# The first input load of a top-2 dispatch kernel, issued as 16 and 112 partitions

## Chip, core and metric

The kernel runs on one core of a Trainium2 chip. A core has five engines, each with its own instruction stream. Three of them matter here: VectorE (DVE), which does all the arithmetic on large tiles; ScalarE (ACT), which computes two sigmoids and issues one store; and SyncE (SP), which computes nothing and issues all the other transfers. A transfer is carried out by 16 DMA engines between HBM and the on-chip memory (SBUF), which has 128 partitions. The metric is device time in microseconds (us) of one execution; lower is better.

## Reference

For each of 16 x 1024 tokens the kernel takes eight router logits, keeps the two largest, turns them into two weights that add up to one, and writes the token's row of 512 floats twice, once scaled by each weight.

```python
def reference(x, router_logits, k):            # x: 16 x 1024 x 512 f32, logits: 16 x 1024 x 8, k = 2
    logits_max = np.max(router_logits, axis=-1, keepdims=True)
    probs = np.exp(router_logits - logits_max)
    probs = probs / np.sum(probs, axis=-1, keepdims=True)
    topk_indices = np.argsort(probs, axis=-1)[..., -k:]
    topk_probs = np.take_along_axis(probs, topk_indices, axis=-1)
    topk_probs = topk_probs / np.sum(topk_probs, axis=-1, keepdims=True)
    x_expanded = x[:, :, np.newaxis, :].repeat(k, axis=2)
    return (x_expanded * topk_probs[..., np.newaxis]).astype(np.float32)
```

The input has 16384 rows of 2 KB (33.6 MB), the output twice as much (67.1 MB), the logits 0.5 MB.

## The kernel before

The 16384 tokens are 128 partitions times 128 rows, in two groups: group 0 has 65 rows in each partition, group 1 has 63 (`GROUPS`). Within a group a partition's rows are neighbours in HBM, so that a load of n rows is, for each partition, one piece of n x 2 KB.

One SBUF buffer, `xs`, holds a group's rows: 65 rows of 512 floats in every partition. A second one, `osp`, holds 18 output rows (each is a pair); at the start it also serves as room for the logits and the work on them. `WA` holds the two weights of every token.

Group 0 is loaded in three transfers of 6, 28 and 31 rows (`LOADS`, line 120). After the first of them the two logits loads are issued (lines 125 and 126), and then the remaining two. All five go out from SP, one behind the other, on SP's DMA queue; none of them waits for anything. Each covers all 128 partitions.

`top2_weights` works on the logits of all tokens at once: a small tournament on DVE (lines 26 to 36), and two sigmoids on ACT of the difference between best and second best (lines 37 and 38). Line 133 then multiplies a block of rows by both weights, into `osp` or into those parts of `xs` whose rows are already used, and line 145 stores the block. The first block is three rows; its store goes out from ACT's queue, all others from SP's. SP's instructions are in program order: five loads, four stores of group 0, three loads of group 1, four stores of group 1. Loads of group 1 wait until the stores that read the same part of `xs` have landed. A multiply waits for its rows' load and for the store that last read its place.

The compiler adds the semaphores. A DMA tells of its landing through one, and there are eight of them that the transfers use in turn.

Of the kernel before, what the change touches and what calls it, by code (L numbers as in the profile page):

```python
# [1 line left out]

# [4 lines left out]

F32 = mybir.dt.float32
ALU = mybir.AluOpType
ACTF = mybir.ActivationFunctionType  # L10
P = 128


def top2_weights(nc, WA, dlt, room, logits, E):

    tt = nc.vector.tensor_tensor
    hi, lo, n = None, None, E  # L20
    while n > 1:
        n //= 2
        if hi is None:
            a, b = logits[:, :, 0:n], logits[:, :, n : 2 * n]
            nhi, nlo = room(n), b
            tt(nhi, a, b, op=ALU.max)  # L26
            tt(nlo, a, b, op=ALU.min)  # L27
        else:
            a, b = hi[:, :, 0:n], hi[:, :, n : 2 * n]
            nhi, nlo, tmp = room(n), room(n), room(n)  # L30
            tt(tmp, lo[:, :, 0:n], lo[:, :, n : 2 * n], op=ALU.max)  # L31
            tt(nlo, a, b, op=ALU.min)  # L32
            tt(nlo, nlo, tmp, op=ALU.max)  # L33
            tt(nhi, a, b, op=ALU.max)  # L34
        hi, lo = nhi, nlo
    tt(dlt, hi[:, :, 0], lo[:, :, 0], op=ALU.subtract)  # L36
    nc.scalar.activation(WA[:, :, 0], dlt, ACTF.Sigmoid, scale=-1.0)  # L37
    nc.scalar.activation(WA[:, :, 1], dlt, ACTF.Sigmoid, scale=1.0)  # L38

GROUPS = [65, 63]

LOADS = [[6, 28, 31], [16, 16, 31]]
BASE = [0, 1]

STORES = [
    [(0, 3, "osp", 0), (3, 15, "osp", 3), (18, 16, "xs", 0), (34, 15, "osp", 0), (49, 16, "xs", 33)],
    [(0, 16, "osp", 2), (16, 16, "xs", 0), (32, 15, "osp", 0), (47, 16, "xs", 32)],
]  # L50

L = 18

FREE = [3, 2]


@with_exitstack
def kernel(
    ctx: ExitStack,
    tc: tile.TileContext,  # L60
    x: bass.AP,
    router_logits: bass.AP,
    k: bass.AP,
    out: bass.AP,
):
    nc = tc.nc
    B, S, D = x.shape
    E = router_logits.shape[-1]
    N = B * S
    assert int(k) == 2 and E == 8 and N == P * sum(GROUPS)  # L70
    M = N // P

    x_v, o_v, rl_v = [], [], []
    t0 = 0
    for n in GROUPS:
        t1 = t0 + P * n
        x_v.append(
            x.rearrange("b s d -> (b s) d")[t0:t1].rearrange("(p m) d -> p m d", p=P)
        )
        o_v.append(  # L80
            out.rearrange("b s k d -> (b s) k d")[t0:t1].rearrange(
                "(p m) k d -> p m k d", p=P
            )
        )
        rl_v.append(
            router_logits.rearrange("b s e -> (b s) e")[t0:t1].rearrange(
                "(p m) e -> p m e", p=P
            )
        )
        t0 = t1  # L90

    wpool = ctx.enter_context(tc.tile_pool(name="wpool", bufs=1))
    xs = wpool.tile([P, max(GROUPS), D], F32)
    osp = wpool.tile([P, L, 2, D], F32)
    WA = wpool.tile([P, M, 2], F32)
    dlt = wpool.tile([P, M], F32)


    flat = osp.rearrange("p l k d -> p (l k d)")
    taken = [0]  # L100

    def room(n):
        o = taken[0]
        taken[0] += M * n
        return flat[:, o : o + M * n].rearrange("p (m n) -> p m n", n=n)

    logits = room(E)

    def place(where, at, n):

        if where == "osp":
            return osp[:, at : at + n]
        return xs[:, at : at + 2 * n, :].rearrange("p (r k) d -> p r k d", k=2)

    m0 = 0
    for g, G in enumerate(GROUPS):
        x0, r = BASE[g], 0
        for n in LOADS[g]:
            tc.keep_in_program_order(
                nc.sync.dma_start(xs[:, x0 + r : x0 + r + n, :], x_v[g][:, r : r + n, :])  # L120
            )
            r += n
            if g == 0 and r == 6:
                n0 = GROUPS[0]
                tc.keep_in_program_order(nc.sync.dma_start(logits[:, :n0], rl_v[0]))  # L125
                tc.keep_in_program_order(nc.sync.dma_start(logits[:, n0:], rl_v[1]))  # L126
                top2_weights(nc, WA, dlt, room, logits, E)
        assert r == G
        for r, n, where, at in STORES[g]:
            og = place(where, at, n)  # L130
            again = where == "osp" and at == 0 and r > 0
            for a, b in [(0, FREE[g]), (FREE[g], n)] if again else [(0, n)]:
                nc.vector.tensor_tensor(  # L133
                    og[:, a:b],
                    xs[:, x0 + r + a : x0 + r + b, :]
                    .unsqueeze(2)
                    .to_broadcast([P, b - a, 2, D]),
                    WA[:, m0 + r + a : m0 + r + b, :]
                    .unsqueeze(3)
                    .to_broadcast([P, b - a, 2, D]),  # L140
                    op=ALU.mult,
                )

            queue = nc.scalar if g == r == 0 else nc.sync
            tc.keep_in_program_order(queue.dma_start(o_v[g][:, r : r + n], og))  # L145
        m0 += G


# [1 line left out]
_INS = ['x', 'router_logits', 'k']  # L150
_OUTS = [((16, 1024, 2, 512), 'float32')]

_NUMBERS = {'k': 2}


# [26 lines left out]
```

## Time and profile before

| What | us |
|---|---|
| median of 3 runs | 239.84 (239.83 to 239.98) |
| the profiled execution's own time | 239.92 |
| its span, from the first to the last instruction | 238.1 |
| DVE busy | 141.9 |
| ACT busy | 1.8 |
| first load: issued at | 0.72 |
| first load: from issue to landing | 6.0 |
| first DVE instruction on logits starts | 8.14 |
| first multiply starts | 12.61 |

The span is what the profile sees of one execution; its own time has 1.8 us more around it. An engine's busy time is the time its instructions ran. For the 16 DMA engines the page gives a share of time in which they had a packet in work, by queue and by slice of the span. A packet is one partition's piece of a transfer: 12 KB in the first load (6 rows), 56 and 62 KB in the next two.

The profile names transfers by the queue that issued them: q1 is SP's, q10 is ACT's.

### The profile page before, as it was taken

How to read it: one execution, taken by the hardware profiler on the slowest of the kernel's cores; microseconds unless marked ns; L12 is line 12 of the kernel's file. 1: busy time of each engine (PE TensorE's matmuls, PEld its weight loads, DVE VectorE, ACT ScalarE, POOL GpSimd, SP SyncE). 2: the span in 40 equal slices, each digit the busy share in tenths (PEclk: the TensorE clock that was granted, in tenths of full speed). 3: DMA queues.
4: the chain of work that ended last, by engine and by line, in shares of the span. 5: the costliest groups of instructions: out<-in, count | busy, mean ns of one | idle time of the engine just before them, and what ended most of it. 6: DMA issues, size and time to landing. Idle time of an engine off the chain costs nothing.

```text
span 238.1 us, 102 instructions
## 1 busy us (share of the span) xinstructions
DVE 141.9 (60%) x22; ACT 1.8 (1%) x3; POOL 0.2 (0%) x4
## 2 busy tenths in 40 slices
DVE  0650499999699999100000699999406999950000
ACT  2000000000000000000000000000000000000000
POOL 0000000000000000000000000000000000000000
DMA  7979998979999999989899999898989999989894
GB/s 265 550 337 500 430 418 374 506 330 495 429 429 407 473 423 402 495 352 528 352 440 435 435 446 501 352 495 374 506 374 462 418 407 451 475 351 517 352 528 176
DMA packets 2448, 101.19 MB, mean 425 GB/s; under 512 B 272, under 2 KB 400, under 8 KB 528
## 3 DMA queue, kind: packets, MB, share of 16 engines
q1 hardware_dynamic: 2304, 99.62, 97.2%
q10 hardware_dynamic: 144, 1.57, 1.5%
HBM read 34.08 MB, written 67.11 MB: 425 GB/s over the span
## 4 chain that ended last, share of the span: by engine, by line
DMA 48%; DVE 40%; SPq 1%; issue 0%; DVEq 0%
DMA xs<-in_x_dram 26%; DVE osp L133 25%; DMA out_dram<-osp 22%; DVE xs L133 14%; SPq L125 0%; SPq L126 0%; SPq L120 0%; SPq L145 0%; DVEq L133 0%
## 5 line engine op out<-in xcount | busy, mean ns | idle before, releaser
L133 DVE TENSOR_TENSOR osp<-xs,WA 128x3072 f32<-128x3072 f32 (+5 forms) x7 | 69.4, 9908 | 61.6 <-DMA xs<-in_x_dram 47.5
L133 DVE TENSOR_TENSOR xs<-xs,WA 128x16384 f32<-128x16384 f32 x4 | 68.9, 17224 | 0.1
L26 DVE TENSOR_TENSOR osp<-osp 128x512 f32<-128x512 f32 x1 | 0.7, 692 | 8.1 <-DMA osp<-in_router_logits_dram 8.1
L37 ACT ACT_TABLE_LOAD x1 | 1.3, 1283 | 0.7 <-PEq L163 0.7
L27 DVE TENSOR_TENSOR osp<-osp 128x512 f32<-128x512 f32 x1 | 0.7, 691 | 0.0
L34 DVE TENSOR_TENSOR osp<-osp 128x256 f32<-128x256 f32 (+1 forms) x2 | 0.7, 352 | 0.0
L32 DVE TENSOR_TENSOR osp<-osp 128x256 f32<-128x256 f32 (+1 forms) x2 | 0.7, 352 | 0.0
L31 DVE TENSOR_TENSOR osp<-osp 128x256 f32<-128x256 f32 (+1 forms) x2 | 0.7, 352 | 0.0
L33 DVE TENSOR_TENSOR osp<-osp 128x256 f32<-128x256 f32 (+1 forms) x2 | 0.7, 351 | 0.0
L37 ACT ACTIVATE WA<-dlt 128x128 f32<-128x128 f32 x1 | 0.3, 314 | 10.1 <-DVE dlt L36 10.1
L36 DVE TENSOR_TENSOR dlt<-osp 128x128 f32<-128x128 f32 x1 | 0.3, 291 | 0.0
L38 ACT ACTIVATE WA<-dlt 128x128 f32<-128x128 f32 x1 | 0.3, 298 | 0.0
L163 POOL MEMSET const-bfloat16-1.0<- 128x1 bf16 x1 | 0.1, 101 | 0.0
L163 POOL MEMSET const-uint8-127<- 128x1 uint8 x1 | 0.1, 101 | 0.0
L163 POOL MEMSET const-float32-0.0<- 128x1 f32 x1 | 0.1, 98 | 0.2 <-issue 0.2
L163 POOL MEMSET const-float32-1.0<- 128x1 f32 x1 | 0.1, 98 | 0.0
## 6 DMA issues: line engine op xcount, KB each, us to landing
out_dram<-osp SPq DMA_DIRECT2D x3, 7680.0 KB, 23.4
xs<-in_x_dram SPq DMA_DIRECT2D x2, 7936.0 KB, 41.7
xs<-in_x_dram SPq DMA_DIRECT2D x2, 4096.0 KB, 40.4
xs<-in_x_dram SPq DMA_DIRECT2D x1, 7168.0 KB, 24.8
xs<-in_x_dram SPq DMA_DIRECT2D x1, 1536.0 KB, 6.0
out_dram<-osp ACTq DMA_DIRECT2D x1, 1536.0 KB, 24.8
osp<-in_router_logits_dram SPq DMA_DIRECT2D x1, 260.0 KB, 6.2
osp<-in_router_logits_dram SPq DMA_DIRECT2D x1, 252.0 KB, 6.4
```

What stands on the lines that cost most here:

```text
L26: tt(nhi, a, b, op=ALU.max)
L27: tt(nlo, a, b, op=ALU.min)
L31: tt(tmp, lo[:, :, 0:n], lo[:, :, n : 2 * n], op=ALU.max)
L32: tt(nlo, a, b, op=ALU.min)
L33: tt(nlo, nlo, tmp, op=ALU.max)
L34: tt(nhi, a, b, op=ALU.max)
L36: tt(dlt, hi[:, :, 0], lo[:, :, 0], op=ALU.subtract)
L37: nc.scalar.activation(WA[:, :, 0], dlt, ACTF.Sigmoid, scale=-1.0)
L38: nc.scalar.activation(WA[:, :, 1], dlt, ACTF.Sigmoid, scale=1.0)
L133: nc.vector.tensor_tensor(og[:, a:b], xs[:, x0 + r + a : x0 + r + b, :] .unsqueeze(2) .to_broadcast([P, b - a, 2, D]), WA[:, m0 + r + a : ...
L163: nc = _bacc.Bacc("TRN2", target_bir_lowering=False, num_devices=1)
```

## The change

The first load of six rows becomes two transfers: one to partitions 0 to 15, then one to partitions 16 to 127. Both go out from SP, in that order, ahead of the logits loads. The other loads are as before.

```diff
         for n in LOADS[g]:
-            tc.keep_in_program_order(
-                nc.sync.dma_start(xs[:, x0 + r : x0 + r + n, :], x_v[g][:, r : r + n, :])
-            )
+
+            parts = [(0, 16), (16, P)] if g == r == 0 else [(0, P)]
+            for p0, p1 in parts:
+                tc.keep_in_program_order(
+                    nc.sync.dma_start(
+                        xs[p0:p1, x0 + r : x0 + r + n, :], x_v[g][p0:p1, r : r + n, :]
+                    )
+                )
             r += n
```

In the built program SP has one instruction more (16 x 3072 and 112 x 3072 elements where 128 x 3072 stood); lines behind it move down by five (133 becomes 138, 145 becomes 150). The order on every engine is otherwise the same. The transfers behind the first use the next semaphore each, and the first multiply, which waited for the one load, waits for the two.

## The prediction, made before the changed kernel was run

> **What bounds the kernel now.** I read the page's DMA part first, since DVE is busy for only 60% of the span.
>
> ```profile
> span 238.1 us, 102 instructions
> ...
> DMA  7979998979999999989899999898989999989894
> ...
> q1 hardware_dynamic: 2304, 99.62, 97.2%
> q10 hardware_dynamic: 144, 1.57, 1.5%
> HBM read 34.08 MB, written 67.11 MB: 425 GB/s over the span
> ```
>
> The reader is to see the two shares: 97.2% + 1.5% = 98.7% of what 16 engines have in 238.1 us, which is 235.0 us of work for each of them. Only 3.1 us are not transfer. Stretches of time (length, then busy time of DVE, ACT and POOL with the count of instructions, clock, DMA share, GB/s) show where those lie:
>
> ```profile
> 0.00:1.73 1.73, 0.00 (x0) 1.01 (x1) 0.20 (x4) 1.00 0.00 0
> 1.73:6.73 5.00, 0.00 (x0) 0.28 (x1) 0.00 (x0) 1.00 0.99 369
> ...
> 60.00:120.00 60.00, 33.78 (x4) 0.00 (x0) 0.00 (x0) 1.00 1.02 443
> 120.00:180.00 60.00, 36.65 (x3) 0.00 (x0) 0.00 (x0) 1.00 1.00 430
> ...
> 237.00:238.10 1.10, 0.00 (x0) 0.00 (x0) 0.00 (x0) 1.00 0.00 0
> ```
>
> Nothing moves before 1.73 us and after 237; in between the share is 1 (a packet counts where it starts, so a stretch can show 1.02). The trace's records of single packets say the same more sharply: first packet at 1.73, last end at 236.94, a mean of 235.11 us of packets on an engine, and 0.09 us per engine in which it had none. So the end is set by 16 engines that never rest: **time = start 1.73 + the packets of the slowest engine + 1.2 for the last landing**. The chain of waits mixes DMA and DVE by turns, and agrees in that each DVE wait in it is for a transfer:
>
> ```profile
> DMA 48%; DVE 40%; SPq 1%; issue 0%; DVEq 0%
> ```
>
> The start, in order of time (start, length, instruction):
>
> ```profile
> 0.72 0.37 SPq L120 DMA_DIRECT2D xs<-in_x_dram  x1
> 1.15 0.43 SPq L125 DMA_DIRECT2D osp<-in_router_logits_dram  x1
> 1.62 0.42 SPq L126 DMA_DIRECT2D osp<-in_router_logits_dram  x1
> 2.09 0.99 SPq L120 DMA_DIRECT2D xs<-in_x_dram  x2
> 8.14 0.69 DVE L26 TENSOR_TENSOR osp<-osp 128x512 f32<-128x512 f32 x1 [8.14 <-DMA osp<-in_router_logits_dram]
> ...
> 12.61 3.36 DVE L133 TENSOR_TENSOR osp<-xs,WA 128x3072 f32<-128x3072 f32 x1 [0.58 <-ACT WA L38]
> ```
>
> All five loads are issued by 3.08, long before the first has landed (0.72 + 6.0 = 6.7). From there the queue is never empty. Each engine has eight 12 KB packets of the first load: the first takes 0.56 to 1.37 us, the other seven 0.46, one every 0.457. Then the logits' packets follow within 10 ns.
>
> **The change, part by part.**
>
> *Removed and added issues.* One SP issue of 0.37 becomes two; the second costs 0.42 (the rows of 0.43 and 0.42 behind the first), and logits and larger loads are issued 0.42 to 0.47 later. The cover is the queue: the logits' packets are wanted at 6.03, and their issue ends at 2.05 now, about 2.5 then. The second part of the first load is wanted sooner. It takes the place of the issue at 1.15; with the first load's distance from issue to first packet, 1.73 - 0.72 = 1.01, its packets can start at 2.16. The engines' first packets end between 2.5 and 3.1. Cost 0. If that cover were gone it would be 0.42.
>
> *Packets.* 128 in both cases, eight for an engine if 16 and 112 partitions are dealt evenly over 16 engines (1 + 7). Bytes are the same. One landing notice more for each engine: the trace has such packets of 4 bytes, 9 ns each. Cost 0.01.
>
> *The added wait* stands at the first multiply (L133, L138 afterwards). It waits till 12.6 for the weights, 5.9 after the load landed; the ten other blocks are queued behind it on DVE, and ACT's store waits for it. With 5.9 us of cover it costs 0; without cover, what the second part is late.
>
> *Which engine writes which partition.* Here I see the only price. Now every transfer of the program spans 128 partitions, and each engine has eight of them; in every such transfer all 16 run together at 12288 B / 460 ns = 26.7 GB/s. The trace cannot tell whose pace that is: the engine's, or that of a lane into the eight partitions it serves. If it is the lane's, a split that makes engines share a lane is paid for. Bounds, from this one row. First part: 16 packets over n lanes take 16/n x 0.457. With n = 16 that is 0.46, as now, and the extra is 0; with sixteen neighbours on two lanes of eight (n = 2) it is 3.66, extra 3.2; with four lanes 1.83, extra 1.37. [...] Second part: shares of seven do not fit lanes of eight, so neighbouring engines meet. Without any meeting the extra is 0; if two engines meet throughout, each of seven packets takes twice as long, extra 7 x 0.457 = 3.2. Each lane's sum over both parts is still eight packets, so it cannot be always; I take the half, 1.6.
>
> [...] By the row of 26.7 GB/s per engine alone, the sum would be 239.9 us.
>
> [...]
>
> *Where the loss goes.* Nothing behind it takes it up, since the engines have 0.09 us of rest. The logits land later, so the weights, the first multiply and ACT's store come later by the same 3 us; the queue still holds the loads of 28 and 31 rows meanwhile. The first SP store is issued at 43.1, when the load of 31 rows has until 47.9 to land (issued at 2.6, 45.3 on its way): 4.8 us of work in hand, which moves along with everything. So the late engine stays late to the end.
>
> *Sum.* 1.37 + 1.6 + 0.01 = 3.0 us. On the profiled execution's own time: 239.92 + 3.0 = 242.9. The median lies 0.08 below that execution: **242.8 us**.
>
> **Rivals.**
>
> *The pace is the engine's own: no change.* For it: one pace in the whole trace, on loads and stores alike (2.42 us for 64 KB is 27.1 GB/s either way). Against it: a pace that an engine and its fixed eight partitions share would look the same. Price 0.01: 239.8 to 239.9. Chance 0.15, with the cases of a few tenths, such as the 0.42 of the second issue if its packets come late.
>
> *Faster: a shorter transfer starts all engines together.* Now the engines' first packets start over some 0.6 us (1.73 to 2.35; the last of them 2.51 if it is a first one). If that is the time in which the descriptors of eight packets for each engine are made out, and one for each comes out sooner, the slowest engine gains up to that spread, less 0.01 and less what the lanes cost. Place: the start of the last engine; price at most -0.6, 239.2; it decides only where lanes cost under 0.1. Against it: the late engine's first packet is short (0.56 at 2.35, against 0.99 at 1.73), so the ends lie closer than the starts, and the landings of the first load are 0.52 apart. It would have to win nearly all of this to pass 0.2%. Chance 0.06.
>
> *The second part waits until the first has landed.* Price: the landing of one packet per engine is 6.0 - 7 x 0.457 = 2.8 us from issue, and the second starts about then anew: +2.8 at most, 242.6. Against it: the logits' packets follow the first load's within 10 ns, on the same queue, before its landing is told. Chance 0.03; in the time it cannot be told from the forecast, in the packets it can.
>
> *One of the two parts only.* The first alone costs 1.4, 241.2; the second alone 1.6, 241.4. Chance 0.22. *Much sharing:* both at their upper ends, 3.2 + 3.2 = 6.4, 246.2; chance of over 244.4: 0.06.
>
> **How the numbers follow.** The forecast (both parts, 2 to 4.5 us) has 0.48. Its own range is 241.8 to 244.4. To take in the cases of one part and of no change, the range goes down to 239.7; below it lie about 0.10, above 244.4 about 0.06. A measurement of this kernel can tell 0.2%, 0.48 us, from no change. Slower by more than that: 0.48 + 0.22 + 0.03 + 0.06 = 0.79; within it 0.15; faster 0.06.
>
> **What would show it.** In the profile after: the first load's two parts land about 1.4 us and 3 us later than 6.7 would have it; the stretch from 1.73 to 6.73 moves well under 369 GB/s; DVE's first instruction starts near 11 instead of 8.1, the first multiply near 15.6; the share of the queues falls little, since slow packets count as busy; 12 KB packets of 0.9 to 1.8 us in the first part, mixed ones in the second, 56 KB packets at the old 2.12 again; from 30 us on everything is the old timeline moved by about 3 us, and the end too. The prediction is wrong if the 12 KB packets stay at 0.46, or if they are slow and the loss is gone before the end: then engines had rest that I have not seen.

## Result, and the profile after

| | before | after |
|---|---|---|
| median, us | 239.93 (239.83 to 240.05, 6 runs) | 241.57 (241.39 to 241.67, 6 runs) |
| ratio to before | 1 | 1.0067, 95% interval 1.0054 to 1.0080 |
| profiled execution: its own time / span | 239.92 / 238.1 | 241.39 / 239.6 |
| first DVE instruction on logits | 8.14 | 10.39 |
| multiply of the second block (15360 elements) | 26.91 | 28.61 |
| multiply of 12288 elements | 66.03 | 67.71 |

The kernel is 1.6 us slower. The page of the changed kernel, its DMA part first:

```profile
span 239.6 us, 105 instructions
...
DMA  7989999897999999798989997989898989999894
...
q1 hardware_dynamic: 2320, 99.62, 97.2%
q10 hardware_dynamic: 144, 1.57, 1.5%
```

The shares are those of before, 98.7% together, but of a longer span: the engines are as full as they were, for 1.5 us more. Slow packets count as busy, so a share cannot show them. Bytes per time can. The same stretch after the first packet as in the prediction (length, busy times, clock, DMA share, GB/s):

```profile
1.73:6.73 5.00, 0.00 (x0) 0.28 (x1) 0.00 (x0) 1.00 1.06 270
```

It moved 270 GB/s where it had been 369, at a DMA share of 1.06. What follows from it, in order of time, after two lines of before that the prediction does not show:

```profile
26.91 16.16 DVE L133 TENSOR_TENSOR osp<-xs,WA 128x15360 f32<-128x15360 f32 x1 [10.94 <-DMA xs<-in_x_dram]
66.03 12.96 DVE L133 TENSOR_TENSOR osp<-xs,WA 128x12288 f32<-128x12288 f32 x1 [2.43 <-DMA out_dram<-osp]
```
```profile
0.73 0.84 SPq L123 DMA_DIRECT2D xs<-in_x_dram  x2
1.62 0.42 SPq L130 DMA_DIRECT2D osp<-in_router_logits_dram  x1
...
10.39 0.69 DVE L26 TENSOR_TENSOR osp<-osp 128x512 f32<-128x512 f32 x1 [10.39 <-DMA osp<-in_router_logits_dram]
...
14.86 3.36 DVE L138 TENSOR_TENSOR osp<-xs,WA 128x3072 f32<-128x3072 f32 x1 [0.58 <-ACT WA L38]
18.25 0.37 ACTq L150 DMA_DIRECT2D out_dram<-osp  x1
28.61 16.16 DVE L138 TENSOR_TENSOR osp<-xs,WA 128x15360 f32<-128x15360 f32 x1 [10.39 <-DMA xs<-in_x_dram]
...
67.71 12.96 DVE L138 TENSOR_TENSOR osp<-xs,WA 128x12288 f32<-128x12288 f32 x1 [2.41 <-DMA out_dram<-osp]
```

Against the table above: the logits are 2.25 us late, the first multiply 2.25, the second one only 1.70, the one at 66 us 1.68. So 2.25 us are lost in the first ten microseconds, and 0.55 of them come back before 28.6. At the end the span is 1.47 longer. The two parts of the load are in the list of issues (KB each, us from issue to landing):

```profile
xs<-in_x_dram SPq DMA_DIRECT2D x1, 1344.0 KB, 7.8
...
xs<-in_x_dram SPq DMA_DIRECT2D x1, 192.0 KB, 3.6
```

Issued at 0.73 and 1.16, they land at 4.4 and 9.0; the one load of before was down at 6.7. In the records of single packets the 12 KB packets of this load take 6.06 us per engine in all instead of 4.23, those of the logits 1.63 instead of 1.34. That is 2.12 of the 2.25 us; the logits' landing is told 0.12 later after them. The packets of the first part are not longer than first packets were before (0.52 to 1.11 us, 0.56 to 1.37 before). What is longer is the packet behind each of them, the first of the second part, with up to 1.32 us. From the second packet of the second part on they are slow nearly evenly, 0.61 to 0.86 us on every engine instead of 0.46.

### The profile page after: what moved, and what is told of

Read it like the earlier page. It is cut to its first block, busy times and chain, and to the rows that moved or that the text cites. A ratio compares the mean times of both kernels' runs of the same rounds, so it can differ in the third digit from the quotient of the medians.

```text
span 239.6 us, 105 instructions
## 1 busy us (share of the span) xinstructions
DVE 141.9 (59%) x22; ACT 1.8 (1%) x3; POOL 0.2 (0%) x4
## 3 DMA queue, kind: packets, MB, share of 16 engines
q10 hardware_dynamic: 144, 1.57, 1.5%
## 4 chain that ended last, share of the span: by engine, by line
DMA 48%; DVE 40%; SPq 1%; issue 0%; DVEq 0%
DMA xs<-in_x_dram 26%; DVE osp L138 25%; DMA out_dram<-osp 22%; DVE xs L138 14%; SPq L123 0%; SPq L131 0%; SPq L130 0%; SPq L150 0%; DVEq L138 0%
```

## Experiments

Twelve runs, one of them the kernel before once more. Each has what each theory expected of it. L: a group of partitions is reached over a lane, and engines that write to one lane share its pace. C: the second transfer itself costs. E: an engine has its own pace whatever it writes to. S: the loss is on the side of HBM. A lane is a way to a group of partitions that the theory assumes; no trace shows one.

Times at the end mix two effects, as will be seen. So here is the early one first: from the first packet to the first DVE instruction on the logits, which waits for all that was queued ahead of it. e3, e4 and e7 move additional bytes. The times of the last column come from several sets of runs with the kernel before in each (240.06 beside e1 to e4, 240.02 beside e5 to e8, 239.93 beside e9 to e12); the ratios below go by those.

| kernel | first packet | DVE starts | between | against before | time, us (median) |
|---|---|---|---|---|---|
| before | 1.73 | 8.14 | 6.41 | | 239.93 |
| e1_rows | 1.73 | 8.29 | 6.56 | +0.15 | 239.90 |
| e4_extra16_spread | 2.08 | 8.96 | 6.88 | +0.47 | 241.00 |
| e3_extra16 | 1.75 | 9.37 | 7.62 | +1.21 | 240.53 |
| after | 1.74 | 10.39 | 8.65 | +2.24 | 241.57 |
| e8_swap | 1.75 | 10.79 | 9.04 | +2.63 | 242.48 |
| e2_halves | 2.05 | 12.11 | 10.06 | +3.65 | 243.30 |
| e7_extra112 | 1.73 | 13.35 | 11.62 | +5.21 | 244.20 |
| e6_eight | 1.75 | 16.64 | 14.89 | +8.48 | 247.37 |

### Is it the second transfer? e1_rows

```diff
-LOADS = [[6, 28, 31], [16, 16, 31]]
+LOADS = [[3, 3, 28, 31], [16, 16, 31]]
```

> The first load in two transfers of three rows each, both over all 128 partitions: as many transfers as in the change, each engine with its own eight partitions in both. Theory L (a pace belongs to a lane into a group of partitions, and engines that share one slow each other): every packet keeps the full pace, so no loss; 6 KB packets at 0.23 to 0.25 us instead of 12 KB at 0.46, one more landing notice: 239.9 to 240.3, DVE starts on the logits at 8.1 to 8.5. Theory C (the second transfer itself costs: its issue of 0.42 us, its landing notice, a break between the transfers): as after, about 241.6, DVE starts near 10.4.

Measured: 239.90 against 240.06 in the same set of runs, ratio 0.9995 (0.9986 to 1.0005).

```profile
1.73:6.73 5.00, 0.00 (x0) 0.28 (x1) 0.00 (x0) 1.00 0.97 353
```
```profile
8.29 0.69 DVE L26 TENSOR_TENSOR osp<-osp 128x512 f32<-128x512 f32 x1 [8.29 <-DMA osp<-in_router_logits_dram]
```

The logits are 0.15 us late instead of 2.25. Two transfers instead of one, each over all 128 partitions, cost nothing here that can be measured in the time. Theory C falls.

### Is it the partitions? e2_halves and e6_eight

```diff
-            parts = [(0, 16), (16, P)] if g == r == 0 else [(0, P)]
+            parts = [(0, 64), (64, P)] if g == r == 0 else [(0, P)]                    # e2_halves
+            parts = [(p, p + 16) for p in range(0, P, 16)] if g == r == 0 else [(0, P)]  # e6_eight
```

> The first load in two transfers, to partitions 0 to 63 and 64 to 127. Theory L, if the two halves have no lane in common: each half has half of the lanes, so four packets on each engine take twice 0.457, first one half and then the other: 7.3 us instead of 3.66, +3.7 at most, less what one buffered packet on each engine saves; 242.5 to 243.6, packets of some 0.9 us. Theory C: as after, 241.6. Theory S (the loss is on the side of HBM: neighbouring rows read together): neighbours in blocks of four instead of seven, about the loss of after or less, 241 to 241.6.

> The first load in eight transfers of 16 neighbouring partitions each. Theory L with four lanes for each sixteen: 128 packets in eight steps of 1.83 us, 14.6 us instead of 3.66; less what the start takes up (some 0.6, as in e3_extra16) and what an engine's buffered packet lets pass: +7 to +11, 247 to 251 us. Theory E (own pace): eight issues of 0.43 us are 3.4 us, about the pace of one packet of 0.457 per engine, so at most +0.5: 239.9 to 240.5.

Measured: 243.30, ratio 1.0131 (1.0116 to 1.0146), and 247.37, ratio 1.0303 (1.0282 to 1.0323). Both lie where L put them, e2 far from what C and S expected and e6 far from E. The buffered packet that both expectations take off for L was my assumption; no run shows one. What the DMA engines moved while only such transfers ran, one stretch of each kernel in the columns of above, first before (whole transfers), then e2_halves, then e6_eight:

```profile
2.70:5.90 3.20, 0.00 (x0) 0.00 (x0) 0.00 (x0) 1.00 1.01 423
```
```profile
2.77:8.93 6.16, 0.00 (x0) 0.00 (x0) 0.00 (x0) 1.00 1.00 222
```
```profile
5.00:11.17 6.17, 0.00 (x0) 0.00 (x0) 0.00 (x0) 1.00 1.02 128
```

The reader is to see the last number beside the one before it: all 16 engines are busy in each, but they move 423 GB/s to 128 partitions, 222 to 64, and 128 to 16 neighbours. In the third of these the 12 KB packets take 1.54 to 1.57 us, 3.4 times the 0.46 of before. The 128 is the rate of a chain of sixteens, not of one alone: the 16 packets of a part start over 1.14 us, so that for most of the time packets of one part and of the next are in work together. No run shows the rate of one sixteen by itself.

### The price of the first part: e3_extra16 and e4_extra16_spread

```diff
+    spare = flat[:, 4096:7168].rearrange("p (n d) -> p n d", d=D)
+    tc.keep_in_program_order(nc.sync.dma_start(spare[0:16], x_v[0][0:16, 0:6, :]))      # e3_extra16
+    tc.keep_in_program_order(nc.sync.dma_start(spare[0:P:8], x_v[0][0:16, 0:6, :]))     # e4_extra16_spread
```

> The kernel before, with the first 196.6 KB loaded once more ahead of it, into spare room of partitions 0 to 15 (the work is otherwise that of before; these 0.2 MB are additional). Theory L with four lanes for these partitions: 1.83 us; 241.4 to 241.8. With theory E (an engine has its pace whatever it writes to) one more packet of 0.457 on each engine: 240.3 to 240.4. With two lanes it would be 3.66: 243.5.

> As e3_extra16, from the same rows of HBM, but into every eighth partition (0, 8, ... 120) instead of partitions 0 to 15. Theory L, if neighbours share a lane in blocks of four and the halves have lanes of their own: eight lanes with two packets each, 0.91 us, 240.8 to 240.9. Theory S (the side of HBM): the same as e3_extra16, since the rows read are the same. Theory E: 240.3 to 240.4, as e3_extra16.

Measured: 240.53, ratio 1.0020 (1.0011 to 1.0029), and 241.00, ratio 1.0041 (1.0027 to 1.0055). Read by their times alone they would speak for E and against L: e3 lies 0.9 us below the 241.4 that L had as its least, and the spread one is the slower. The table shows why that reading is wrong. First e3, then e4:

```profile
0.73 0.39 SPq L116 DMA_DIRECT2D osp<-in_x_dram  x1
...
9.37 0.69 DVE L26 TENSOR_TENSOR osp<-osp 128x512 f32<-128x512 f32 x1 [9.37 <-DMA osp<-in_router_logits_dram]
```
```profile
0.73 0.58 SPq L116 DMA_DIRECT2D osp<-in_x_dram  x1
...
3.95 0.33 SPq L127 DMA_DIRECT2D osp<-in_router_logits_dram  x1
...
8.96 0.69 DVE L26 TENSOR_TENSOR osp<-osp 128x512 f32<-128x512 f32 x1 [8.96 <-DMA osp<-in_router_logits_dram]
```

From the first packet to the logits, e3 loses 1.21 us and e4 0.47: the same rows of HBM, only other partitions, and 0.74 us between them (0.41 if counted from the start of the span, since e4's first packet comes later). The packets say the same: nine of 12 KB take 5.42 us per engine in e3 and 4.74 in e4; the eight of before took 4.23. That rules S out. The 0.74 is near half of the 1.54 that a packet takes in e6's chain, which is what L would save with the eight lanes in the place of four that the expectations assume; no run counts lanes. e4 reaches no more than the 0.46 that one more packet per engine costs anyway. Its logits were issued only at 3.95, just after the additional transfer had landed at 3.93; the engines still had packets of the first load till 6.8, so this cost nothing. Two things then turn the times round: SP took 0.58 us for e4's first issue instead of 0.39, and its first packet came 0.33 later; and e3 got a part back that e4 did not get, which is the subject of the last five runs.

Of 1.21 us, 0.46 are the packet itself. So sixteen neighbours cost the first part some 0.75 us more than a packet here, not the 1.54 - 0.46 = 1.08 of e6_eight's chain. Some of it may lie under the engines' first packets, which in the kernel before take about 0.95 instead of 0.46 anyway.

### The price of the second part: e7_extra112 and e8_swap

```diff
+    tc.keep_in_program_order(nc.sync.dma_start(spare[16:P], x_v[0][16:P, 0:6, :]))       # e7_extra112
-            parts = [(0, 16), (16, P)] if g == r == 0 else [(0, P)]
+            parts = [(16, P), (0, 16)] if g == r == 0 else [(0, P)]                     # e8_swap
```

> The kernel before, with rows of partitions 16 to 127 loaded once more ahead of it, into spare room of the same partitions (additional work of 1.38 MB). Own pace, theory E: seven packets of 0.457 on each engine, 3.2 us, 243.2. Theory L: shares of seven meet on lanes of eight; from the 4.3 to 4.7 us that the second part took in the profile of after instead of 3.2, 1.1 to 1.5 us more: 244.2 to 244.8, less some 0.6 that the start takes up and less a stretch of 0.5 of slow packets if it is missing: 243.4 to 244.6.

> The two parts of the change in the other order: partitions 16 to 127, then 0 to 15. Theory L: the second part's meeting costs as before (1.1 to 1.5), the sixteen neighbours 1.4 less what engines that finish early take up; the start hides nothing of them now. Logits land at 9.5 to 10.8 instead of 8.0, 241.0 to 242.2. If the loss came from a small transfer at the very start (theory R: the engines' start-up), the swap would lose nothing: 239.9 to 240.3, logits at 8.1 to 8.5.

Measured: 244.20, ratio 1.0171 (1.0156 to 1.0186), and 242.48, ratio 1.0101 (1.0084 to 1.0118; of its four runs the profiled one, which the table shows, took 241.79, the others 242.48 to 242.62).

```profile
13.35 0.69 DVE L26 TENSOR_TENSOR osp<-osp 128x512 f32<-128x512 f32 x1 [13.35 <-DMA osp<-in_router_logits_dram]
```

This is e7. It loses 5.21 us ahead of the logits, of which 3.20 are its seven packets: the 112 partitions alone cost 2.0 us more than their bytes, above the 1.1 to 1.5 expected. e8 was expected to have its logits at 9.5 to 10.8, and they landed at 10.69; its time is 0.3 above what was expected. A small transfer at the very start is not the cause, theory R falls; by the profiled executions the order matters by 0.4 us at the logits. 0.75 and 2.0 are more than the 2.24 that both parts cost together in the changed kernel, so the two overlap by some 0.5 us, if each costs in the changed kernel what it costs alone.

### What comes back: e5_again, e9_delay04, e10_delay12, e11_sp_store, e12_sp_store_after

In the kernel before, the 56 KB packets of the load of 28 rows take 2.116 us each, except in a stretch between 17.7 and 26 us, where they take up to 2.57; over the load that is 0.58 us per engine too much. In the changed kernel it is 0.07.

> The kernel before once more, to see what of its trace comes back. In the first profile the 56 KB packets that start at 17.7 to 24 us took 0.55 us per engine more than the 2.116 of the others; in the profile of after, and in those of e2_halves and e3_extra16, none did. If that stretch belongs to the kernel before, it is there again, with 0.4 to 0.6 us; if it comes and goes by chance, it may be missing, and the span is then some 0.5 us shorter (237.6).

Measured: 0.44 us too much in that load, at the same place, and 0.12 in the next. The stretch belongs to the kernel before. (The execution took 240.56, with a span of 238.8, for another reason: the last landings are 1.3 us apart, 0.66 in the first profile; why is not known.)

The next guess was that the stretch hangs on the moment at which ACT's first store comes in between the loads.

```diff
+    idle = room(2)
+    tt(idle, logits[:, :, 0:2], logits[:, :, 2:4], op=ALU.max)          # e9_delay04
+    idle = room(E)
+    tt(idle, logits, logits, op=ALU.max)                               # e10_delay12
-            queue = nc.scalar if g == r == 0 else nc.sync
+            queue = nc.sync                                            # e11 (from before), e12 (from after)
```

> The kernel before with one more DVE instruction of 0.42 us ahead of the work on the logits (its result isn't used); the first block's store on ACT's queue then goes out about 0.35 us later, at 16.35. In the traces so far the stretch of slow 56 KB packets (0.4 to 0.5 us per engine, from 17.7 to 26) is there in the four runs in which this store is issued 8.56 to 8.60 us after those packets begin, and missing in the six with 8.68 to 8.96. Theory T (it depends on when the store comes in between the loads): with some 8.95 the stretch is gone, 239.4 to 239.6, although the kernel does more. Theory U (the stretch goes where shared lanes have shifted the engines against each other at the start, whatever the store does): it stays, 239.9 to 240.1.

> As e9_delay04 with one DVE instruction of 1.1 to 1.2 us: the store goes out near 17.2. Theory T: the stretch is gone unless a later moment is as bad, 239.4 to 239.7. Theory U: it stays, 239.9 to 240.1.

> The kernel before with the first block's store on SP's queue, behind the loads of 28 and 31 rows, instead of on ACT's queue between them. Theory T: no store comes in between the loads, no slow stretch, 239.3 to 239.6. Theory U: the stretch stays in the loads, 239.9 to 240.1.

> The changed kernel with the first block's store on SP's queue. By theory T the slow stretch, of which the changed kernel had none, is what gave back a part of the 2.25 us that its logits came late. Then without such a store in both kernels the whole price shows: this one is 241.5 to 241.7, and 1.9 to 2.3 us above e11_sp_store. By theory U the difference to e11_sp_store stays 1.5 to 1.7.

Measured: e9 240.19, ratio 1.0007 (0.9998 to 1.0016); e10 239.88, ratio 1.0005 (0.9987 to 1.0023). The store went out at 16.46 and 17.22 instead of 16.00, and the stretch stays, with 0.60 and 0.55 us. In e9 the store comes 8.99 us after those packets begin (mean of the engines), in e7, which has no such stretch, 8.96. So the moment does not decide, and theory T falls.

e11 took 240.32, ratio 1.0012 (1.0003 to 1.0021), e12 241.67, ratio 1.0066 (1.0053 to 1.0078). e11 lies outside of what both theories expected (239.3 to 239.6 and 239.9 to 240.1). They tell where the stretch sits. Three instructions of each, in order of time, first e11 (not split), then e12 (split):

```profile
8.18 0.69 DVE L26 TENSOR_TENSOR osp<-osp 128x512 f32<-128x512 f32 x1 [8.18 <-DMA osp<-in_router_logits_dram]
...
25.04 16.16 DVE L133 TENSOR_TENSOR osp<-xs,WA 128x15360 f32<-128x15360 f32 x1 [9.03 <-DMA xs<-in_x_dram]
...
66.58 12.96 DVE L133 TENSOR_TENSOR osp<-xs,WA 128x12288 f32<-128x12288 f32 x1 [4.85 <-DMA out_dram<-osp]
```
```profile
10.76 0.69 DVE L26 TENSOR_TENSOR osp<-osp 128x512 f32<-128x512 f32 x1 [10.76 <-DMA osp<-in_router_logits_dram]
...
27.62 16.16 DVE L138 TENSOR_TENSOR osp<-xs,WA 128x15360 f32<-128x15360 f32 x1 [9.03 <-DMA xs<-in_x_dram]
...
68.09 12.96 DVE L138 TENSOR_TENSOR osp<-xs,WA 128x12288 f32<-128x12288 f32 x1 [3.79 <-DMA out_dram<-osp]
```

The difference is 2.58 us at the logits, still 2.58 at the second multiply, and 1.51 at 66 us. Without a store among the loads nothing comes back in the load of 28 rows (e11 has no slow packet in it). It comes back later, at the end of the load of 31 rows, where the store is now queued: there e11's packets are 1.06 us too slow per engine, e12's 0.04. At the end 240.32 and 241.67 are 1.35 apart, less than either theory had: U expected 1.5 to 1.7, T 1.9 to 2.3.

So this much is shown: a kernel whose first transfers ran at full pace loses 0.45 to 1.06 us per engine in the loads of 28 and 31 rows, where its loads first meet a store (seven runs, counting e4_extra16_spread, whose additional transfer cost no more than its packet), and one whose first transfers had slow packets loses 0.06 to 0.11 there (seven runs). Why is not shown. At the logits, the landings of the second kind are told 0.51 us after the engines start on the next load (means over 16 engines), those of the first kind 0.39 to 0.42, and those of e4 0.46. So e4 stands between the two and yet loses as much as the first kind: the runs do not show that this lead decides.

No kernel here is measurably faster than the one before; e1_rows is equal to it.

## Why the prediction was right

It said 242.8, slower, within 239.7 to 244.4; it is 241.57. The direction was right, and so was the place of the loss, the packets of the two parts; the size was not: 1.6 us instead of 3.0. The forecast's own range began at 241.8, and the stated range reaches below it only to take in the cases of one part and of no change. By its time alone the result would look like the case of the second part only (241.4). That it lies within the range is thus luck in part: both parts do cost (e3, e7), but they overlap, and a third of the loss comes back.

The steps, in its order:

- **The bound.** Right: the queues' shares are unchanged while the packets' time per engine grows by 1.56 us (235.11 to 236.67) and the span by 1.47.
- **The issue, the landing notice and the wait at nothing.** Right: e1_rows has as many issues and landing notices as the changed kernel (288 packets of 4 bytes, 272 before) and costs nothing. The second part's issue at 1.16 was early enough: the first engine is through with the first part at 2.35, and the next packet starts at 2.38. The first multiply still starts right behind the weights, 0.58 us after DVE's last work on them, as before.
- **The lanes.** Right that the partitions set a price: with transfers to 128, 64 and sixteen neighbouring partitions the same 16 engines moved 423, 222 and 128 GB/s, and with the sixteen spread the additional load cost 0.47 us instead of 1.21 (e4, e3). Lanes themselves, how many there are and how fast one is, no run shows. I had 1.83 us for a packet of sixteen neighbours, and in e6's chain it takes 1.54.
- **The first part's 1.37.** It rests on four lanes for sixteen neighbours, which was my assumption; no run shows the term. What the runs showed in its place is less: 1.08 in e6's chain, some 0.75 at the start of the kernel (e3). The first packets take 0.95 us on average in the kernel before too, and that a part of the price can lie under this was not in the sum. Nor were the packets of the first part themselves 0.9 to 1.8 us long, as I had expected; those behind them were, 0.61 to 1.32 us.
- **The second part's 1.6.** Too little: 2.0 by itself (e7). That shares of seven meet on lanes, from which the 1.6 comes, no run shows either. Sum at the logits: predicted 3.0, measured 2.25, with an overlap of some 0.5 that I had not counted.
- **"Nothing behind it takes it up."** This is the step that failed. I read the 0.09 us without a packet as no rest at all, and did not look at how long the packets take over the whole run. The kernel before has 0.58 us of slow packets in one load, the changed one 0.07; with them, 0.19 us that come back over the loads of group 1 (1.68 late at 98 us, 1.49 at 134) and smaller ones, 2.25 us at the logits become 1.5 in the span. e12 against e11 shows that this give-back does not belong to the load of 28 rows: it moves with the place where the first store meets the loads. I had named such a loss that is gone before the end as a sign of being wrong; a third of it was gone.
- **"The late engine stays late to the end."** There was none: the engines end the second part within 0.62 us of each other (0.46 for the first load before), and the last landings are 0.48 us apart, 0.66 before.

## What to carry to other kernels

With every DMA engine busy, transfers to 64 neighbouring partitions moved 222 GB/s here, and a chain of sixteens 128, where whole ones moved 423. Split by rows, the load cost nothing measurable (239.90 us against 240.06 beside it), split by partitions 1.6 us: in a kernel that lives on its DMA queues, split a load by rows rather than by partitions. The queues' share was 98.7% before and after and did not show the loss; bytes per time (369 and 270 GB/s) and the time of equal packets (4.23 and 6.06 us per engine) did. And before a loss is carried to the end of the sum, look for packets in the old trace that are longer than their equals: they can be room in which a delay vanishes, as a part of it did here (some 0.5 of 2.25 us by the second multiply).

## What the runs showed of the hardware

- With all 16 engines busy, transfers to all 128 partitions moved 423 GB/s, to 64 neighbours 222, and to sixteen neighbours, one sixteen after the other, 128.
- Sixteen partitions in a row cost more than sixteen spread ones: the same 196.6 KB cost 0.74 us less from the first packet to the logits (0.41 less from the start of the span) when every eighth partition was written (e4) instead of partitions 0 to 15 (e3).
- The slow packets where loads first meet a store, 0.45 to 1.06 us per engine, and next to none of them (0.06 to 0.11) after a start with slow packets.
- In e6_eight SP issued the first logits load at 4.60, just after the first of the eight parts had landed at 4.58, and the second at 6.14, after the next had landed at 6.12: in the traces of before and after the transfers tell their landings on eight semaphores in turn, the ninth on the first one's again, so I put the wait down to that. The engines had packets all the while, so it cost nothing here.
